# Thirty-two bytes in front of the activations: the activations stand 96 bytes from the weights, modulo 256, in place of 64

## The chip, the cores and the metric

One core of one Trainium2 chip runs the kernel. The metric is the device time of one execution in microseconds (us); less is better. All times below are of this one core.

## What is computed

The reference is a stack of four transformer-like layers in float32 on 256 tokens of 1024 channels. Two layers of a first kind mix tokens by a retention, a short convolution and a 31-tap convolution; two of a second kind mix by an mLSTM, a sparse attention and a differential attention. Each mixes through gates, and each is followed by a gated feed-forward block. Cut to what matters here:

```python
for l in range(2):                                # first kind
    h = rmsnorm(x, norm_mix_pre[l])
    proj = h @ w_in[l]                            # 1024 x 7168
    ...                                           # three branches, each ends in a 512 x 1024 product
    x = x + rmsnorm(merged @ w_o[l], norm_mix_post[l])
    h = rmsnorm(x, norm_ffn_pre[l])
    up = causal_dwconv(h @ w_up[l], ffn_conv_w[l])
    f = (silu(gate) * val) @ w_down[l]            # 2816 x 1024
    x = x + rmsnorm(f, norm_ffn_post[l])
for l in range(2):                                # second kind, likewise
    ...
```

Nearly all of the work is products of activations with weights that are each used once.

## The kernel before

**The stream of weights.** All weight matrices are cut on the host into blocks of 128 x 128 and packed, in the order of use, into chunks of eight blocks (512 KB). SyncE loads a chunk into a tile `wraw` (four buffers). A float32 weight goes to the tensor engine as the sum of two parts in the format float32r: ScalarE rounds the chunk into `whi` (line 326), and VectorE subtracts to get the rest into `wlo` (line 415, called from `Weights.ensure`). `whi` and `wlo` have four buffers each.

**The products.** `Gen.job` runs one product of the plan. For a weight block (kind "B") the weights are stationary (128 x 128) and 256 tokens of activations are moving. Activations have two parts too, so a block costs three matmuls: hi x `whi`, lo x `whi`, hi x `wlo`, all recorded under line 403. Activations are `hh`, `hl` (a whole normed input), `yh`, `yl` (a branch's output, or the first part of a norm), `fh`, `fl` (the feed-forward's middle) and `ckh`, `ckl` (a low-rank input of the sparse attention). A few products (kind "A") have the roles exchanged: the activations are stationary and 512 columns of weights move. Where `job` meets a chunk that is not split (`yw`, `wraw`), and in the sums of squares (`sqt`, `ones`, `cst`), the operands are plain float32.

**Work beside the products.** Generators (`spawn`, `side`) issue the attention, convolution and norm steps between the products. The program's order is fixed when it is built.

**Where tiles lie.** Each tile pool takes a stretch of every partition's memory, in the order in which pools are made, and a tile starts at the next multiple of 32 bytes. The pool `weights` is first, then `consts`, then `state` (the pool `self.xpool`), and behind these come the pools of each stage. In the built program all buffers of `wraw`, `whi` and `wlo` start at 128 modulo 256 bytes, and `x`, `yh`, `yl`, `sqt`, `hh`, `hl`, `fh` and `fl` at 192. Inside a tile, a token tile is 1024 bytes long and a weight block 512, so that the distance from a stationary block of weights to the activations that move against it is 64 bytes modulo 256 in every matmul on these tiles. `ckh` and `ckl` start at 32; their distance from the weights is 160.

```python
self.wpool = ctx.enter_context(tc.tile_pool(name="weights", bufs=1))
self.cpool = ctx.enter_context(tc.tile_pool(name="consts", bufs=1))
self.xpool = ctx.enter_context(tc.tile_pool(name="state", bufs=1))
...
self.x = self.xpool.tile([P, KD, T], F32, name="x")
...
todo = [(0, 0), (0, 1), (1, 0)] if len(ws) == 2 else [(0, 0)]
for j, (a, b) in enumerate(todo):
    self.mm(o, ws[a], xs[b], start=j == 0 and k == 0 and t % 2 == 0,
```

Of the kernel before, what the change touches and what calls it, by code (L numbers as in the profile page):

```python
# [11 lines left out]
F32 = mybir.dt.float32  # L12
# [5 lines left out]
P = 128  # L18
# [28 lines left out]
# norms after which the first chunks of weights and what they meet go unsplit  # L47
WHOLE = (1, 2, 3, 4)
# tiles of a product that ends a chain, the last ones apart
COLUMNS = ((0, 2), (2, 2), (4, 2), (6, 1), (7, 1))  # L50
# gates and products of the branches, in their order
# [8 lines left out]
def ffn_up(arr, l):  # L60
    """Gate and value tiles side by side; the first two products take four tiles."""
    t = [[_cols(i * P, P), _cols(FF + i * P, P)] for i in range(KF)]
    return [(arr, (l,), "B", KD, c) for c in [t[0] + t[1], t[2] + t[3]] + t[4:]]


def plan():
    """The weights in the order in which the tensor engine takes them: (array, index, kind,
    k tiles, columns), kind "B" by column tiles of 128 and "A" by rows of 512."""
    jobs = []

    def seg(arr, idx, nk, off, n, step=256):
        for i in range(0, n, step):
            jobs.append((arr, idx, "B", nk, [_cols(off + i + j, P) for j in range(0, step, P)]))

    def last_singly(arr, idx, nk):
        seg(arr, idx, nk, 0, D - 256)
        seg(arr, idx, nk, D - 256, 256, P)

    for l in range(DEPTH):
        seg("w_in", (l,), KD, OFF1["cfb"], 512, 512)  # L80
        seg("w_in", (l,), KD, OFF1["cfa"], 512, 512)
        for s, n in (("q", 256), ("k", 256)):
            seg("w_in", (l,), KD, OFF1[s], n)
        jobs.append(("w_in", (l,), "A", KD, _cols(OFF1["v"], 512)))
        for s, n in (("scc", 512), ("scx", 512), ("scb", 512), ("g", 512)):
            seg("w_in", (l,), KD, OFF1[s], n)
        for what, b in BRANCHES1:
            if what == "g":
                seg("w_in", (l,), KD, OFF1["gate"] + b * D, D)
            else:  # L90
                seg(("w_ret_out", "w_sc_out", "w_cf_out")[b], (l,), 4, 0, D)
        last_singly("w_o", (l,), KD)
        jobs += ffn_up("w_up", l)
        last_singly("w_down", (l,), KF)
    for l in range(DEPTH):
        w = "w_in_2"
        misc = np.full(P, -1)
        misc[:64] = _cols(OFF2["ik"], 64)
        misc[64:72] = _cols(OFF2["mif"], 8)
        misc[72:76] = _cols(OFF2["iw"], 4)  # L100
        jobs.append((w, (l,), "B", KD, [_cols(OFF2[s] + j, P) for s in ("iq", "ckv") for j in (0, P)]))
        seg(w, (l,), KD, OFF2["mqk"], 512, 512)
        jobs.append((w, (l,), "B", KD, [misc]))
        seg(w, (l,), KD, OFF2["mqk"] + 512, 512)
        jobs.append((w, (l,), "A", KD, _cols(OFF2["mv"], 512)))
        seg(w, (l,), KD, OFF2["mo"], 512)
        seg(w, (l,), KD, OFF2["dq"], 512)
        seg(w, (l,), KD, OFF2["dk"], 512)
        jobs.append((w, (l,), "A", KD, _cols(OFF2["dv"], 512)))
        seg("dsa_w_kv_up_2", (l,), 2, 0, 512)  # L110
        jobs.append(("dsa_w_kv_up_2", (l,), "A", 2, _cols(512, 512)))
        seg(w, (l,), KD, OFF2["sq"], 512)
        for what, b in BRANCHES2:
            if what == "g":
                seg(w, (l,), KD, OFF2["gate"] + b * D, D)
            else:
                seg("w_branch_2", (l, b), 4, 0, D)
        seg("w_out_2", (l,), KD, 0, D)
        jobs += ffn_up("w_gate_up_2", l)
        if l + 1 < DEPTH:  # L120
            seg("w_down_2", (l,), KF, 0, D)
        else:
            last_singly("w_down_2", (l,), KF)
    return jobs
# [48 lines left out]
def pack_params(inputs=None):  # L173
    """Per-channel parameters, channels on partitions: (offsets, array)."""
    off, parts = {}, []
# [37 lines left out]
def make_consts():  # L213
    """Tables that depend on shapes alone: (offsets, array [128, n])."""
    off, parts = {}, []
# [55 lines left out]
def whole_chunks():  # L271
    """The chunks that go to the tensor engine as float32, unsplit."""
    out, n, i = set(), 0, 0
    for _, _, kind, nk, cols in plan():
        if kind == "B" and len(cols) == 4:
            if i // 2 in WHOLE:
                out.add(n // CB)
            i += 1
        n += nk * (len(cols) if kind == "B" else 4)
    return out  # L280


class Weights:
    """The stream of weights: loads ahead, then each chunk as the sum of two float32r parts."""
# [13 lines left out]
    def cuts(self, c):  # L298
        """The first chunk comes in halves."""
# [44 lines left out]
class Gen:  # L344
    SLACK = 4000

    def __init__(self, ctx, tc, aps):
# [15 lines left out]
        self.idle = None  # L363
        self.x = self.xpool.tile([P, KD, T], F32, name="x")
# [82 lines left out]
    def split(self, hi, lo, src):  # L447
        """src as the sum of its float32r rounding and of the exact rest."""
# [3 lines left out]
    def behind(self, engine):  # L452
        """What is traced here is issued after the engine's last urgent instruction."""
# [21 lines left out]
    def side(self):  # L475
        """Steps of the tasks beside the products, as far as the vector engine keeps up."""
# [13 lines left out]
    def job(self, evac, mov, needs=(), scale=None, last=False, spare=None):  # L490
        """The next product of the plan. mov(k) gives the two parts of the activations' tile k;
        scale, per token, is for activations that were not normalised yet; spare gives tiles."""
# [3 lines left out]
        if kind == "B":  # L496
            n = len(cols)
            accs = [self.acc() for _ in range(-(-n // 2))]
            if self.idle is not None:
                # only to keep the tensor engine's clock up while it waits  # L500
# [4 lines left out]
            for k in range(nk):  # L505
                xs = mov(k)
                for t in range(n):
# [4 lines left out]
                    # a start clears the marks of its whole bank: the first product of a bank has it  # L512
# [32 lines left out]
    def swap(self, out, src):  # L545
        """src with the halves of each 64 channels exchanged"""
# [3 lines left out]
    def rows(self, r):  # L550
        # r in DRAM, from where a row goes to many partitions
# [4 lines left out]
    def spread(self, out, row):  # L556
        """a row on all the partitions of out"""
        self.nc.sync.dma_start(out, row.to_broadcast(list(out.shape)))

# [31 lines left out]
    def rstd(self, pool, ps, scale, name):  # L591
        """1 / sqrt(scale * ps + eps)"""
# [6 lines left out]
    def sumsq(self, out, last, hold):  # L599
        """Over channels, on every partition: the sum of the squares of the eight tiles, which it  # L600
        takes by pairs, the last two also one by one (send). The first ones are added up before.
        With hold the tensor engine gets them together at the end."""
# [37 lines left out]
    def start_norm(self, g, l, folded=4):  # L640
        """Takes x by pairs of tiles (feed) for a norm whose scale per token comes last."""
# [20 lines left out]
    def end_norm(self, sd=None):  # L662
        """What the first products take, with their scale, and what the others take."""
# [38 lines left out]
    def branches(self, order, bufs, pool, mov, gate_load, needs, ys, done):  # L702
        """The sum over branches of gate * (branch output times its matrix), as two parts. A gate
        sigmoid(z) comes as tanh(z / 2), its double less 1."""
# [31 lines left out]
    def post_norm(self, zg, sums, gpre, l):  # L736
        """x += normalised zg; then the next norm's input. With s the root mean square of z, what
        the norm sees is u = s * x + zg, s times the new x."""
# [23 lines left out]
    def unscale(self, sd):  # L762
        """x out of u"""
# [10 lines left out]
    def out_proj(self, mov, g, l):  # L774
        """Four products whose columns are scaled by g, with the sum of their squares."""
# [11 lines left out]
    def first_mix(self, l, norm):  # L787
        dmov, rs, whole, mov = norm
        nc = self.nc
        with ExitStack() as st:  # L790
# [6 lines left out]
            def new_y(b):  # L797
                """Buffers for a branch's output, once those of the one before last are free."""
# [13 lines left out]
            # conformer convolution  # L812
# [65 lines left out]
            # retention  # L878
# [44 lines left out]
            # short convolution  # L923
# [133 lines left out]
    def residual(self, mov, gpre, l):  # L1057
        """x += four products; then the next norm's input."""
# [17 lines left out]
    def second_mix(self, l, norm):  # L1076
        dmov, rs, whole, mov = norm
        nc = self.nc
        with ExitStack() as st:
# [11 lines left out]
            def new_y(b):  # L1091
                """Buffers for a branch's output, once those of the one before last are free."""
# [14 lines left out]
            def rope(o):  # L1107
                """Rotates two tiles in place."""
# [6 lines left out]
            # indexer  # L1115
# [63 lines left out]
            # key/value rank  # L1179
# [33 lines left out]
            def q_task(sqs, dst, rq):  # L1213
                """rotation of the queries, and their scale per token and head"""
# [39 lines left out]
            # mLSTM queries and keys  # L1254
# [29 lines left out]
            # mLSTM gates  # L1284
# [102 lines left out]
            # attention with a softmax: sets of (queries, keys) of 64 channels  # L1387
            def softmax_group(q, k, rq, t, grp, bias, p, sums):
                """p = exp(scores - max) for the queries of tile t, sums its row sums. A group is
                sets in the same half of the partitions, one a tile."""  # L1390
# [22 lines left out]
            def transposed(p):  # L1413
                """p by keys: for each set its blocks of keys"""
# [18 lines left out]
            def ahead(q, k, rq, t, bias):  # L1433
                """The groups of tile t with their softmax, one group ahead."""
# [49 lines left out]
            def diff(l=l):  # L1484
                init = 0.8 - 0.6 * math.exp(-0.3 * l)
                for t in range(2):
                    yt = tl([P, 512], "yt", tag="yt", bufs=3)
                    for (half, tiles), p, sums in ahead(dq, dk, rq_d, t, None):
# [5 lines left out]
                        # both maps in one, up to the first one's sums  # L1494
# [44 lines left out]
            # differential attention  # L1539
# [22 lines left out]
            # sparse attention: keys and values out of the rank  # L1562
# [72 lines left out]
```

## Time and profile before

| | before |
|---|---|
| time, median of 3 runs | 1789.86 us (1789.58 to 1791.06) |
| span of the profiled execution | 1789.1 us |
| granted TensorE clock, mean | 1.000 of full speed |
| PE (matmul) busy | 1777.4 us, 99% of the span |
| PEld (weight load) busy | 1729.2 us, 97% |
| VectorE (DVE) busy | 1363.0 us, 76% |
| ScalarE (ACT) busy | 1111.0 us, 62% |
| DMA | 322.52 MB, mean 180 GB/s |

The span runs from the first to the last instruction of one profiled execution; it lies 0.8 us under the median of the runs. A matmul's record lasts longer than the time until the next one starts, since matmuls are pipelined; what counts in a stretch is how many fit into it.

### The profile page before, as it was taken

The page shows a single profiled execution, that of the slowest core. Times are in us where ns is not written, and L with a number is a line of the kernel's source. Part 1 is how long each engine was busy: PE and PEld are TensorE (multiplying, and loading weights), DVE is VectorE, ACT ScalarE, POOL GpSimd, SP SyncE. Part 2 cuts the span into 40 slices and gives each one's busy share as a digit, 9 for nine tenths or more (in the row PEclk, how much of TensorE's full clock was granted, in tenths as well). Part 3 has the DMA queues.
Part 4 walks back from the last instruction along what each step waited for, and adds up shares of the span by engine and source line. Part 5 has one row for each costly group of instructions (what it writes and reads, how often), then busy time and mean ns, then how long its engine had stood idle before and what let it go on. Part 6 is the DMA issues. An engine that isn't in the chain of part 4 may idle for free.

```text
span 1789.1 us, 35765 instructions
## 1 busy us (share of the span) xinstructions
PE 1777.4 (99%) x14462; PEld 1729.2 (97%) x14462; DVE 1363.0 (76%) x2082; ACT 1111.0 (62%) x1787; POOL 70.2 (4%) x144
## 2 busy tenths in 40 slices
PE   8999999999999999999999999999999999999999
PEld 8999999999999999999998999999999999999999
DVE  8988679865999769884887877865569887677553
ACT  7575468755666567765576666654457666655542
POOL 0000000000000000000022100000000310000000
PEclk9999999999999999999999999999999999999999
DMA  7555546554655546555465644565555664356663
GB/s 265 191 171 179 187 154 200 188 187 164 210 168 188 177 138 204 189 189 188 137 195 177 201 142 139 168 207 194 189 186 180 199 201 139 124 177 200 193 196 132
DMA packets 94648, 322.52 MB, mean 180 GB/s; under 512 B 12257, under 2 KB 16913, under 8 KB 94482
## 3 DMA queue, kind: packets, MB, share of 16 engines
q1 hardware_dynamic: 91010, 314.15, 53.9%
q0 software_dynamic: 3328, 6.09, 1.1%
q8 instruction: 113, 1.85, 0.4%
q14 instruction: 53, 0.43, 0.1%
q10 hardware_dynamic: 144, 0.00, 0.0%
HBM read 312.80 MB, written 1.10 MB: 175 GB/s over the span
## 4 chain that ended last, share of the span: by engine, by line
PE 97%; DVE 1%; DMA 1%; issue 0%; ACT 0%; POOL 0%; SPq 0%; DVEq 0%; ACTq 0%; POOLq 0%
PE acc L403 90%; PE sp L403 6%; PE sp L408 1%; DMA tmp<-dq 0%; DMA Wm<-rows 0%; DMA x<-x 0%; DVE wlo L415 0%; DVE sc L1167 0%; DVE x L415 0%; DVE m L1166 0%; DVE yw L420 0%; ACT sd L445 0%; DVE dq L415 0%; ACT whi L326 0%; POOL tmp L548 0%
## 5 line engine op out<-in xcount | busy, mean ns | idle before, releaser
L326 ACT ACTIVATE whi<-wraw 128x1024 fp32r<-128x1024 f32 (+1 forms) x575 | 606.7, 1057 | 535.9 <-PE acc L403 367.8
L415 DVE TENSOR_TENSOR wlo<-wraw,whi 128x1024 fp32r<-128x1024 f32 (+1 forms) x575 | 699.0, 1220 | 282.9 <-ACT whi L326 281.3
L403 PE MATMUL acc<-hh,whi 128*128 128x256 f32 x2832 | 791.4, 280 | 0.0
L403 PE MATMUL acc<-hl,whi 128*128 128x256 f32 x2832 | 790.8, 280 | 0.0
L403 PE MATMUL acc<-hh,wlo 128*128 128x256 f32 x2832 | 789.9, 280 | 0.0
L403 PEld LDWEIGHTS acc<-hh,whi 128*128 128x128 f32 x2832 | 531.0, 188 | 5.5 <-issue 3.7
L403 PEld LDWEIGHTS acc<-hl,whi 128*128 128x128 f32 x2832 | 531.7, 188 | 1.9 <-issue 1.2
L403 PEld LDWEIGHTS acc<-hh,wlo 128*128 128x128 f32 x2832 | 531.4, 188 | 1.1 <-issue 0.8
L403 PE MATMUL acc<-yh,whi 128*128 128x256 f32 x1280 | 269.7, 284 | 6.2 <-ACT whi L326 6.2
L403 PE MATMUL acc<-yh,wlo 128*128 128x256 f32 x832 | 231.3, 283 | 0.0
L403 PEld LDWEIGHTS acc<-yh,whi 128*128 128x128 f32 x1280 | 210.5, 190 | 7.1 <-ACT whi L326 6.2
L403 PE MATMUL acc<-fh,wlo 128*128 128x256 f32 x704 | 196.0, 278 | 0.0
L403 PE MATMUL acc<-fl,whi 128*128 128x256 f32 x704 | 195.6, 278 | 0.0
L403 PE MATMUL acc<-fh,whi 128*128 128x256 f32 x704 | 195.5, 278 | 0.0
L403 PEld LDWEIGHTS acc<-yh,wlo 128*128 128x128 f32 x832 | 155.8, 189 | 0.4
L403 PEld LDWEIGHTS acc<-fh,wlo 128*128 128x128 f32 x704 | 132.3, 188 | 0.0
L403 PEld LDWEIGHTS acc<-fl,whi 128*128 128x128 f32 x704 | 132.2, 188 | 0.0
L403 PEld LDWEIGHTS acc<-fh,whi 128*128 128x128 f32 x704 | 132.0, 188 | 0.0
L403 PE MATMUL acc<-yl,whi 128*128 128x256 f32 x384 | 108.2, 282 | 0.0
L403 PEld LDWEIGHTS acc<-yl,whi 128*128 128x128 f32 x384 | 72.1, 188 | 0.2
L445 ACT ACT_TABLE_LOAD x50 | 64.2, 1283 | 5.5 <-DVE Wm L426 3.0
L420 DVE SCALAR_TENSOR_TENSOR up<-z,prm,up 128x254 f32<-128x254 f32 (+1 forms) x128 | 55.3, 479 | 0.0
(282 smaller groups left out, 1815.2 us busy)
## 6 DMA issues: line engine op xcount, KB each, us to landing
wraw<-stream SPq DMA_DIRECT2D x581, 512.0 KB, 3.6
kr<-rows SPq DMA_DIRECT2D x32, 64.0 KB, 3.0
dec<-decay SPq DMA_DIRECT2D x2, 768.0 KB, 4.3
x<-x SPq DMA_DIRECT2D x4, 256.0 KB, 6.3
rf<-rows SPq DMA_DIRECT2D x8, 128.0 KB, 3.5
tmp<-dq POOLq DMA_DIRECT2D x16, 64.0 KB, 3.8
Wm<-rows SPq DMA_DIRECT2D x8, 128.0 KB, 3.6
tmp<-dk POOLq DMA_DIRECT2D x16, 64.0 KB, 3.9
```

The costliest lines, as they stand in the source:

```text
L326: nc.scalar.activation(h[:, s], r[:, s], AF.Copy)
L403: return self.nc.tensor.matmul(out, lhsT, rhs, start=start, stop=stop, **kw)
L408: return self.nc.tensor.transpose(out, in_, self.c("ident")[:k, :k])
L415: self.recent = self.nc.vector.tensor_tensor(out=out, in0=a, in1=b, op=op)
L420: return self.nc.vector.scalar_tensor_tensor(out, a, s, b, op0=op0, op1=op1)
L445: return self.nc.scalar.activation(out, in_, f, **kw)
```

## The change

A tile of 8 float32 numbers (32 bytes in each partition) is allocated at the start of the pool `state`, in front of `x`. Nothing writes or reads it. Comments and docstrings go at the same time, which leaves the built instructions alone.

```diff
@@ -361,6 +361,8 @@
         self.t_x = [None]
         self.urgent = {}
         self.idle = None
+
+        self.xpool.tile([P, 8], F32, name="xpad")
         self.x = self.xpool.tile([P, KD, T], F32, name="x")
         xin = aps["x"].rearrange("p (k t) -> p k t", k=KD)
         self.coff, nco, _ = make_consts()
```

In the two built programs every engine has the same instructions in the same order, on tiles of the same shapes; only addresses differ. The weights, `cst`, `prm` and `ones` stay where they were. Everything from `x` on, in the pool `state` and in the pools behind it, lies 32 bytes further on. So `x`, `yh`, `yl`, `sqt`, `hh`, `hl`, `fh`, `fl` start at 224 modulo 256 and move against weights at a distance of 96; `ckh` and `ckl` start at 64, a distance of 192. With the roles exchanged (kind "A") the weights, moving, lie 192 bytes (modulo 256) from `hh` and `hl` before and 160 after, and from `ckh` and `ckl` 96 before and 64 after.

## Rows read from the trace of the kernel before

**Rows 1.** The page: busy time, and the chain that ended last.
```profile
PE 1777.4 (99%) x14462; PEld 1729.2 (97%) x14462; DVE 1363.0 (76%) x2082; ACT 1111.0 (62%) x1787; POOL 70.2 (4%) x144
...
PE 97%; DVE 1%; DMA 1%; issue 0%; ACT 0%; POOL 0%; SPq 0%; DVEq 0%; ACTq 0%; POOLq 0%
PE acc L403 90%; PE sp L403 6%; PE sp L408 1%; DMA tmp<-dq 0%; DMA Wm<-rows 0%; DMA x<-x 0%; DVE wlo L415 0%; DVE sc L1167 0%; DVE x L415 0%; DVE m L1166 0%; DVE yw L420 0%; ACT sd L445 0%; DVE dq L415 0%; ACT whi L326 0%; POOL tmp L548 0%
```

**Rows 2.** Groups of matmuls: count, busy us, mean ns of one, idle before.
```profile
L403 PE MATMUL acc<-hh,whi 128*128 128x256 f32 x2832 | 791.4, 280 | 0.0
...
L403 PE MATMUL acc<-yh,whi 128*128 128x256 f32 x1280 | 269.7, 284 | 6.2 <-ACT whi L326 6.2
L403 PE MATMUL acc<-yh,wlo 128*128 128x256 f32 x832 | 231.3, 283 | 0.0
L403 PE MATMUL acc<-fh,wlo 128*128 128x256 f32 x704 | 196.0, 278 | 0.0
...
L403 PE MATMUL acc<-yl,whi 128*128 128x256 f32 x384 | 108.2, 282 | 0.0
```

**Rows 3.** Four windows of 160 us, one in each feed-forward: busy us (instructions), clock, DMA.
```profile
core 0: us, PE busy (x) PEld busy (x) DVE busy (x) ACT busy (x) POOL busy (x), PEclk, DMA share, GB/s
253.00:413.00 160.00, 160.00 (x1361) 160.00 (x1360) 128.73 (x203) 112.66 (x191) 0.00 (x0) 1.00 0.58 190
700.00:860.00 160.00, 159.75 (x1333) 158.66 (x1332) 117.71 (x185) 107.31 (x185) 0.42 (x3) 1.00 0.55 179
1152.00:1312.00 160.00, 160.00 (x1414) 160.00 (x1413) 99.17 (x130) 82.83 (x118) 0.00 (x0) 1.00 0.62 196
1620.00:1780.00 160.00, 160.00 (x1414) 160.00 (x1413) 93.19 (x115) 75.85 (x104) 0.00 (x0) 1.00 0.59 187
```

**Rows 4.** Windows of PE alone: the eight stretches at the denser pace, and their sum.
```profile
17.50:25.00 7.50, 7.50 (x68) 1.00 0.59 191
...
1150.30:1316.90 166.60, 166.60 (x1472) 1.00 0.61 195
1343.60:1353.80 10.20, 10.20 (x93) 1.00 0.52 157
1613.00:1785.10 172.10, 172.10 (x1521) 1.00 0.57 184
sum 373.10, PE 373.10; mean PE 46.64
```

**Rows 5.** Timeline of PE where a dense stretch begins: start us, length us, what.
```profile
1149.34 1.03 PE L403 MATMUL sp<-sqt,ones 128*128 128x256 f32 x4
1150.02 0.58 PE L403 MATMUL acc<-yh,whi 128*128 128x256 f32 x2
1150.43 0.28 PE L403 MATMUL acc<-yh,wlo 128*128 128x256 f32 x1
```

**Rows 6.** Timeline of PE: a product on `ckh` and `ckl`, 160 bytes from the weights.
```profile
1433.87 0.28 PE L403 MATMUL acc<-ckl,whi 128*128 128x256 f32 x1
...
1435.06 0.28 PE L403 MATMUL acc<-ckh,wlo 128*128 128x256 f32 x1
1435.18 0.39 PE L403 MATMUL acc<-whi,ckh 128*128 128x512 f32 x1
```

**Rows 7.** Timeline of PE just ahead of that: short plain float32 products in a row.
```profile
1430.73 1.17 PE L403 MATMUL sp<-mv,Wm 128*128 128x129 f32 x9
1431.83 1.89 PE L403 MATMUL sp<-sqt,cst 128*8 128x256 f32 x8
```

**Rows 8.** Groups that prepare the weights, and what ended their waits.
```profile
L415 DVE TENSOR_TENSOR wlo<-wraw,whi 128x1024 fp32r<-128x1024 f32 (+1 forms) x575 | 699.0, 1220 | 282.9 <-ACT whi L326 281.3
L326 ACT ACTIVATE whi<-wraw 128x1024 fp32r<-128x1024 f32 (+1 forms) x575 | 606.7, 1057 | 535.9 <-PE acc L403 367.8 <-issue 125.8 <-DMA wraw<-stream 14.4
```

## The prediction

> **What bounds the kernel now.** I read the page first: PE is busy for 99% of the span, and the chain that ended last is PE for 97%, of which products with weights (`acc`, line 403) are 90% [rows 1]. So the time is the number of these matmuls times the pace at which they follow each other, and little else. The groups give the number: 2832 for each of three pairs on `hh` and `hl`, 704 for each of three on `fh` and `fl`, and 1280 + 832 + 384 on `yh` and `yl`, together 3 x 2832 + 3 x 704 + 2496 = 13,104 matmuls of 256 columns in float32r [rows 2].
>
> Next I asked whether they all run at one pace, with windows of one length laid into long unbroken products. They don't. A window of 160 us in the first feed-forward holds 1361 matmuls, in the third and fourth 1414 [rows 3]. A row counts every instruction that touches the window, and one lasts 0.28 us [rows 2], so two or three of each count belong to the edges. The paces are 160 / (1361 - 2.4) = 117.8 ns and 160 / (1414 - 2.4) = 113.35 ns. I call them slow and fast. PE is busy throughout in both, weight loads too, and the granted clock is 1.00, the 2.4 GHz level, in both. VectorE (129 against 99 us busy) and ScalarE are less loaded in the fast ones, but they hold up nobody there: the matmul groups on `hh` and `fh` have no idle time before them [rows 2, 3]. The DMA moves 196 GB/s in a fast window and 190 in a slow one, so it is no brake either.
>
> The third view is where the fast pace stands. Eight stretches have it, 373.1 us in all; two feed-forwards hold nearly everything (166.6 and 172.1 us), and within a stretch it never changes [rows 4]. It begins after an interruption: at 1149.34 us a sum of squares with plain float32 operands cuts the row of products, and what follows it is fast [rows 5]. 373.1 / 0.11335 = 3290 matmuls are fast; some 9,800 are not.
>
> So the same instruction, on tiles at the same distance modulo 256, settles into one of two rhythms and keeps it until something breaks in. Matmul and weight load run side by side, both read the same memory, and a rhythm that depends on the moment of restart looks like two streams of reads that get in each other's way more or less often. That is an inference; no row names a collision.
>
> **The change, part by part.** It removes nothing and adds no instruction. The order on every engine is that of before, so nothing is moved past a queue and no wait is added.
>
> The new tile costs no time: it has no instruction, and the highest tile still fits.
>
> All other engines' operands from `x` on lie 32 bytes further on. I price that at nothing: VectorE and ScalarE have 24% and 38% of the span free [rows 1], and the two steps in front of PE, the split of a chunk, wait for each other and for PE most of the time (283 us and 536 us idle ahead of them) [rows 8]. If a slower access made each 1% longer, the 699 us of `wlo` would grow by 7 us, spread over idle time; without that cover it would cost the 7 us.
>
> What is left is the distance of the moving activations from the stationary weights, 64 before and 96 after, in all 13,104 matmuls. No row has activations that move at 96 from the weights, so I bound the price by the paces that the trace shows.
> - The fast pace everywhere: 9,800 x (117.8 - 113.35) = 43.6 us less.
> - The slow pace everywhere: 3290 x 4.45 = 14.6 us more.
> - A third distance is in the trace. Eleven gaps on `ckh` and `ckl`, at 160, take 1435.18 - 1433.87 = 1.31 us, or 119 ns each [rows 6]. With this pace everywhere, 14.6 + 13,104 x 1.3 = 32 us more.
> - Weight loads alone set a floor. Nine short float32 products with a new stationary block each take 1.17 us, the last one 0.28 of it, so (1.17 - 0.28) / 8 = 111 ns [rows 7]. Below this none of these products can go, since each has its own weight load. At the floor everywhere: 43.6 + 13,104 x 2.3 = 74 us less.
>
> Plain float32 products of 256 columns go at (1.89 - 0.38) / 7 = 216 ns [rows 7], about half the rate of float32r; I leave them out of the sum, and with them the few products of 512 columns.
>
> The rule of the Trainium skill that speaks against the change is in "TensorE: Matmul & The Clock Gate", step-by-step part, on the weight load: the engine has two independent read ports, so "Loading the next tile's weights doesn't steal SBUF read bandwidth from the running matmul." By it no distance matters, and the sum is zero. The same page's isolated gap for 256 columns, 262 cycles at 2.4 GHz or 109 ns, would as an estimate make the products 13,104 x 7.5 = 98 us shorter than they are. The trace sides with neither figure: it has two paces, both longer.
>
> Which pace will 96 have? The trace shows that distance matters at all only through 64 (two paces) and 160 (one, slower, in few and short products), and a straight line between the two would put 96 at 117.4 ns, a little worse than today's mean of (3290 x 113.35 + 9,814 x 117.8) / 13,104 = 116.7. I don't take the line, because the paces go by steps: a stretch is fast or slow and never between. At 64 the kernel sits where a restart decides, and 32 bytes are 32/1024 of a moving operand, 113.35 x 32 / 1024 = 3.5 ns of its stream. That is most of the 4.45 ns between the rhythms, so I expect the new distance to have one rhythm nearly everywhere, not a mix. The fast one is 2 ns off the floor of the weight loads, that is, a rhythm in which hardly anything collides; and the moving stream, which passes through 1024 bytes while the weights pass through 512, starts with half as much lead again at 96. I take the fast one, by judgement more than by proof.
>
> The sum: 43.6 us, less some 4 us for the 3% of the chain that isn't PE, for products next to a break, and for the first mixes, where VectorE has little room and at a faster pace would be waited for. 40 us off a span of 1789.1 gives 1749, and with 0.8 us around it 1750 us. The median of the runs is 0.8 us above the profiled span, within the spread of the runs.
>
> **The rivals.**
> - *It ends slower: a worse rhythm everywhere.* Place: the same products. Price: 14.6 us at 117.8 ns, 32 us at the 119 ns of distance 160, thus 1804 to 1822 us. For it: 75% of the matmuls are at the slow pace today, and the only other distance seen is worse. Against it: those are 11 gaps after a break. It decides if fewer than a quarter of the products are fast. Chance 0.25.
> - *The mix is dealt anew.* The restart goes on deciding, and other stretches turn out fast. Each of the four feed-forwards is worth about 1500 x 4.45 = 6.7 us, so the time goes in such steps from 1804 to some 1770 us. For it: at 64 it is just so. Chance 0.18: 0.08 of it faster, 0.05 the same, 0.05 slower.
> - *The distance does nothing,* by the rule above: two independent read ports, and the two rhythms come from something else that the change leaves alone. 1790 us. For it: breaks are in the same places. Against it: `ckh` at another distance has a third pace. Chance 0.05.
> - *No collisions are left,* and the products run near the floor of the weight loads: 1716 us. For it: the fast pace is already within 2.3 ns. Against it: no float32r product in the trace does so. Chance 0.10.
>
> **How the numbers follow.** The forecast has 0.42 and gives 1750 us (its own range, from 1746 with no haircut to 1768 with half of the slow products turned fast). Faster by over 0.2% (3.6 us, about what a measurement of this kernel can tell) is 0.42 + 0.08 + 0.10 = 0.60; within 0.2%: 0.05 + 0.05 = 0.10; slower: 0.25 + 0.05 = 0.30. The range goes from 1735, between the full fast rhythm and the floor, to 1806, just past the slow rhythm everywhere. Outside lie most of the floor case and the half of the slower rival that follows distance 160, together about 2 in 10.
>
> **What would show it.** Right: windows of 160 us in the first and second feed-forward hold 1400 matmuls or more, at unchanged clock; the mean of a matmul on `hh` falls from 280 ns towards 276; no new wait in front of PE. Wrong in size: some of these windows still hold 1361. Wrong in sign: the third and fourth feed-forward hold 1361 or fewer. Wrong in mechanism: the counts are as before and the time has changed elsewhere, in waits of PE for `whi`, or on VectorE. The products on `ckh`, at 192 after, should change their 119 ns too if the distance is what matters.

## The result, and the profile after

The changed kernel takes 1831.86 us (median of 4 runs, 1831.44 to 1832.37), the kernel before 1789.72 us beside it (4 runs, 1789.53 to 1791.06). The ratio is 1.0234, with a 95% interval of 1.0221 to 1.0246. The change makes the kernel 42.1 us slower. That is above the range of the prediction, and on the side of its first rival.

The page of the kernel after: span, busy time, and the chain that ended last.

```profile
span 1830.2 us, 35765 instructions
...
PE 1818.8 (99%) x14462; PEld 1771.1 (97%) x14462; DVE 1364.6 (75%) x2082; ACT 1110.7 (61%) x1787; POOL 69.4 (4%) x144
...
PE 97%; DVE 1%; DMA 1%; ACT 1%; issue 0%; POOL 0%; SPq 0%; DVEq 0%; ACTq 0%; POOLq 0%
```

Against [rows 1], only PE's two rows moved, by 41.4 and 41.9 us. VectorE and ScalarE are busy for as long as before, on the addresses 32 bytes further on, and the chain is PE for 97% still. So the loss is inside PE's products.

The costliest groups of the kernel after. Line 403 of before is line 405 now, and line 415 is 417.

```profile
L326 ACT ACTIVATE whi<-wraw 128x1024 fp32r<-128x1024 f32 (+1 forms) x575 | 606.6, 1056 | 579.5 <-PE acc L405 396.9
L417 DVE TENSOR_TENSOR wlo<-wraw,whi 128x1024 fp32r<-128x1024 f32 (+1 forms) x575 | 698.4, 1218 | 316.1 <-ACT whi L326 314.2
L405 PE MATMUL acc<-hh,whi 128*128 128x256 f32 x2832 | 800.1, 283 | 0.0
...
L405 PE MATMUL acc<-yh,whi 128*128 128x256 f32 x1280 | 274.2, 286 | 6.6 <-ACT whi L326 6.6
```

The steps in front of PE last as long as in [rows 8] (1056 against 1057 ns, 1218 against 1220 ns), and their idle time has grown by 44 and 33 us, most of it waiting for PE or for each other. PE waits for `whi` about as long as before (6.6 against 6.2 us in [rows 2]). A matmul on `hh` has gone from 280 to 283 ns.

Four windows of 160 us, one in each feed-forward of the kernel after (busy us and instructions of each engine, clock, DMA):

```profile
core 0: us, PE busy (x) PEld busy (x) DVE busy (x) ACT busy (x) POOL busy (x), PEclk, DMA share, GB/s
260.00:420.00 160.00, 160.00 (x1336) 160.00 (x1335) 126.56 (x202) 111.28 (x189) 0.00 (x0) 1.00 0.56 184
705.00:865.00 160.00, 160.00 (x1336) 160.00 (x1335) 118.79 (x184) 107.94 (x183) 0.00 (x0) 1.00 0.57 188
1185.00:1345.00 160.00, 160.00 (x1334) 159.94 (x1333) 87.36 (x108) 75.84 (x106) 0.00 (x0) 1.00 0.56 185
1650.00:1810.00 160.00, 160.00 (x1336) 160.00 (x1335) 89.57 (x112) 74.38 (x104) 0.00 (x0) 1.00 0.55 185
```

Against 1361, 1333, 1414 and 1414 in [rows 3], the count is now 1334 to 1336 in all four: 160 / (1336 - 2.4) = 120.0 ns for each matmul, at the same granted clock. (The 1333 of before is a window with a break in it, of which its 158.66 us of weight loads tell.) The two rhythms are gone. One has taken their place, and it is worse than either.

To check this on all of them, I took the time from each start to the next start for every pair of neighbouring float32r matmuls of 256 columns in the trace, 12,868 pairs without those next to a break. The mean is 116.64 ns before and 119.97 after. 12,868 x 3.33 ns = 42.8 us, against 42.1 us measured: this is the whole difference. I call this mean the pace below.

The products on `ckh`, whose distance went from 160 to 192, as a timeline of PE in the kernel after:

```profile
1462.55 0.29 PE L405 MATMUL acc<-ckl,whi 128*128 128x256 f32 x1
...
1462.90 0.28 PE L405 MATMUL acc<-ckl,whi 128*128 128x256 f32 x1
...
1463.70 0.28 PE L405 MATMUL acc<-ckh,wlo 128*128 128x256 f32 x1
1463.81 0.39 PE L405 MATMUL acc<-whi,ckh 128*128 128x512 f32 x1
```

The same eleven gaps as in [rows 6] take 1463.81 - 1462.55 = 1.26 us, or 115 ns each, where [rows 6] has 119; the last eight of them take 1463.81 - 1462.90 = 0.91 us, or 114 ns each. The same 32 bytes made these products faster while they made the others slower. So it looks like the distance 96 that is slow, and 192 may be good.

### The profile page after: what moved, and what is told of

Read it like the earlier page. It is cut to its first block, busy times and chain, and to the rows that moved or that the text cites. A ratio compares the mean times of both kernels' runs of the same rounds, so it can differ in the third digit from the quotient of the medians.

```text
span 1830.2 us, 35765 instructions
## 1 busy us (share of the span) xinstructions
PE 1818.8 (99%) x14462; PEld 1771.1 (97%) x14462; DVE 1364.6 (75%) x2082; ACT 1110.7 (61%) x1787; POOL 69.4 (4%) x144
## 4 chain that ended last, share of the span: by engine, by line
PE 97%; DVE 1%; DMA 1%; ACT 1%; issue 0%; POOL 0%; SPq 0%; DVEq 0%; ACTq 0%; POOLq 0%
PE acc L405 90%; PE sp L405 6%; PE sp L410 1%; DMA tmp<-dq 0%; DMA x<-x 0%; DMA Wm<-rows 0%; DVE sc L1169 0%; ACT L447 0%; ACT whi L326 0%; DVE x L417 0%; DVE m L1168 0%; DVE yw L422 0%; ACT sd L447 0%; DVE wlo L417 0%; DVE dq L417 0%
## 5 line engine op out<-in xcount | busy, mean ns | idle before, releaser
L326 ACT ACTIVATE whi<-wraw 128x1024 fp32r<-128x1024 f32 (+1 forms) x575 | 606.6, 1056 | 579.5 <-PE acc L405 396.9
L417 DVE TENSOR_TENSOR wlo<-wraw,whi 128x1024 fp32r<-128x1024 f32 (+1 forms) x575 | 698.4, 1218 | 316.1 <-ACT whi L326 314.2
L405 PE MATMUL acc<-hh,whi 128*128 128x256 f32 x2832 | 800.1, 283 | 0.0
L405 PE MATMUL acc<-hh,wlo 128*128 128x256 f32 x2832 | 798.7, 283 | 0.0
L405 PE MATMUL acc<-yh,whi 128*128 128x256 f32 x1280 | 274.2, 286 | 6.6 <-ACT whi L326 6.6
L405 PE MATMUL acc<-yl,whi 128*128 128x256 f32 x384 | 108.8, 284 | 0.0
```

The source lines that it names most:

```text
L326: nc.scalar.activation(h[:, s], r[:, s], AF.Copy)
L405: return self.nc.tensor.matmul(out, lhsT, rhs, start=start, stop=stop, **kw)
L417: self.recent = self.nc.vector.tensor_tensor(out=out, in0=a, in1=b, op=op)
```

## The experiments

My theory after the result: the pace belongs to the distance between the stationary block and the moving operand, modulo 256 bytes, and 96 is among the worst. The rivals: it is the address of the activations themselves; or it is what other engines and the DMA do at the new addresses while PE runs.

**Everything shifted.** The 32 bytes go in front of the weights in place of the activations. All tiles then lie where they lie after the change, except that the weights have moved along, so that the distance is 64 again.

```diff
         self.wpool = ctx.enter_context(tc.tile_pool(name="weights", bufs=1))
+        self.wpool.tile([P, 8], F32, name="wpad")
 ...
-        self.xpool.tile([P, 8], F32, name="xpad")
```

> The 32 bytes stand in front of the weights instead of the activations: all tiles move by 32, the activations stand at 224 modulo 256 as in the change, but their distance from the weights is 64 again. If the distance sets the pace: 1790 us, as before, with the two rhythms of 113.3 and 117.8 ns back in the same stretches. If what costs is that the activations start at an odd multiple of 32 bytes, whatever the weights do: 1832 us and 120 ns throughout, as in the change.

Measured: 1790.43 us (10 runs), ratio to before 0.9999 (0.9990 to 1.0008). The windows of [rows 3] laid over this kernel, PE alone (busy us and instructions, clock, DMA):

```profile
253.00:413.00 160.00, 160.00 (x1361) 1.00 0.57 190
700.00:860.00 160.00, 159.75 (x1331) 1.00 0.52 178
1152.00:1312.00 160.00, 160.00 (x1415) 1.00 0.58 196
1620.00:1780.00 160.00, 160.00 (x1415) 1.00 0.58 187
```

Both rhythms are back, and in the same feed-forwards. The addresses by themselves cost nothing. The distance does.

**The same distance, 256 bytes further.** The pad is `[P, 72]`, 288 bytes.

> The unused tile has 288 bytes: a distance of 96 plus 256 from the weights. If only the distance modulo 256 counts: 1832 us and 120 ns, as with 32 bytes. If it is the distance itself, or the place of the activations in a larger unit, another pace, with 1790 us as likely as anything.

Measured: 1832.63 us (1831.82 to 1833.70), ratio 1.0236 (1.0221 to 1.0251), pace 119.97 ns. It is the changed kernel's time again, so the distance counts modulo 256, or modulo something that divides it.

**The other distances.** The pad is 128, 96, 64, 192, 160 or 224 bytes, for distances of 192, 160, 128, 0, 224 and 32; the edit is the one number in `[P, 8]`.

> The unused tile has 128 bytes: a distance of 192. With the change the low-rank products on ckh came to a distance of 192 and went at 113.3 ns. If the distance sets the pace of every float32r product alike: 113.3 ns nearly throughout, about 1790 - 43 = 1747 us. If the address of the activations alone counts (64 modulo 256, an even multiple of 32): as before, 1790 us.

> The unused tile has 96 bytes: a distance of 160. Before the change the low-rank products on ckh stood at 160 and went at 119 ns. If the distance sets the pace: 119 ns throughout, 1790 + 13100 x 2.3 ns = 1820 us. If an odd multiple of 32 bytes is what costs: 120 ns and 1832 us as in the change, the two lie within 0.7%, so the pace in the windows decides.

> The unused tile has 64 bytes: a distance of 128. Distances 64 and 192 have the same two rhythms (113.3 and 117.8 ns), 96 and 160 don't. If multiples of 64 share them: some 1770 to 1790 us, windows with one or the other rhythm. If the paces repeat after 128 bytes only, 128 is a new class with 0, its pace open (111 to 122 ns, 1716 to 1860 us) but the same as that of distance 0.

> The unused tile has 192 bytes: a distance of 0, both operands at 128 modulo 256. If the paces repeat after 128 bytes: the time of distance 128, within 1%. If they repeat after 256 only: any other. A plain picture of two streams that start at the same place and collide there would make it the slowest of all, over 1832 us.

> The unused tile has 160 bytes: a distance of 224, 32 short of 256. If the paces repeat after 128 bytes: 120.0 ns and 1832 us, as at 96. If they mirror (32 bytes on either side alike): as at 32, whatever that is. If the odd multiple of 32 is what costs: 119 to 120 ns, 1814 to 1832 us.

> The unused tile has 224 bytes: a distance of 32. If the paces repeat after 128 bytes: 118.8 ns and 1814 us, as at 160. If odd multiples of 32 cost alike: between 1814 and 1832 us. If neither: another time, and the paces depend on the distance modulo 256 without a shorter period.

| distance | time, us (median) | ratio to before (95%) | pace, ns | by pace, us |
|---|---|---|---|---|
| 0 | 1831.37 | 1.0230 (1.0215 to 1.0245) | 119.94 | 1832 |
| 32 | 1791.49 | 1.0008 (0.9998 to 1.0017) | 116.80 | 1792 |
| 64 (before) | 1789.72 | 1 | 116.64 | 1790 |
| 96 (after) | 1831.86 | 1.0234 (1.0221 to 1.0246) | 119.97 | 1833 |
| 128 | 1822.83 | 1.0182 (1.0165 to 1.0199) | 119.24 | 1823 |
| 160 | 1813.60 | 1.0126 (1.0109 to 1.0143) | 118.82 | 1818 |
| 192 | 1779.52 | 0.9943 (0.9929 to 0.9958) | 115.86 | 1780 |
| 224 | 1811.31 | 1.0118 (1.0103 to 1.0133) | 118.32 | 1811 |

The last column is 1789.9 + 12,868 x (pace - 116.64 ns). It meets the profiled run of every kernel within 2 us (at 160 that run took 1818.2 us, the slowest of its four), so nothing but the pace is needed for any of them. The table has no shorter period: 32 and 160 differ by 22 us, 96 and 224 by 21. (0 and 128 lie within the 1% that was set beforehand; they differ in their rhythms, 120.0 ns alone at 0, 118.7 and 120.0 ns at 128.) It has no simple slope either. At 0, 96 and 224 I find one rhythm, and at 32 one but for two short stretches at 117.8 ns; at 64, 128, 160 and 192 there are several, and a stretch keeps the one that it fell into. At 192 neither time that was expected came: the rhythms are the two of distance 64, in other places. The windows of that kernel, PE alone:

```profile
253.00:413.00 160.00, 160.00 (x1360) 1.00 0.55 188
680.00:840.00 160.00, 160.00 (x1361) 1.00 0.56 190
1140.00:1300.00 160.00, 160.00 (x1414) 1.00 0.60 194
1600.00:1760.00 160.00, 160.00 (x1361) 1.00 0.54 186
```

One of the four is fast here, two of them in [rows 3]. The kernel is 10 us faster than before all the same, since more of its other products are fast.

**PE alone.** This kernel, like the next three, computes nothing of the reference: it runs matmuls on float32r tiles while ScalarE, VectorE and the DMA have nothing to do. Weights and activations start at the same place modulo 256, and the moving operand is taken `d` bytes in. Each distance comes three times, each time after a break of a few plain float32 products; then come turns (odd matmuls with weights at distance 64, even ones at 0), 512 columns, and plain float32.

```python
for turn in range(3):
    for d in range(0, 256, 32):
        rest(4 + turn)
        o = acc(f"at{d}b")
        for i in range(120):
            k, b = i % 5, i % 15
            mm(o[:, :T], w[:, b * P:(b + 1) * P], a[:, d // 4 + k * T:d // 4 + k * T + T])
```

> Nothing of the reference is computed: after one load and four copies the tensor engine runs alone, with no work of ScalarE, VectorE or the DMA beside it. Runs of 120 float32r matmuls of 256 columns at each of the eight distances, three restarts each, then matmuls whose weights stand in turn at 64 and 0, then 512 columns, then plain float32. If the paces are an affair of weight load and moving operand: the paces of the eight kernels come back, 120.0 ns at 0 and 96, 113.3 or 117.8 at 64 and 192, 118.3 at 224, 116.7 at 32, 118.5 or 120 at 128, 117.5 to 120 at 160. If other engines' reads and writes or the DMA make the second party: one pace at all distances, the floor near 111 to 113 ns. In the turns: if a matmul is slowed by the weights that load beside it, those on weights at 64 (beside a load at 0) are longer than those on weights at 0; if by its own weights, the other way round. Plain float32: 216 ns at all distances.

Windows of 12 us of this kernel, PE alone. In order: distances 64, 96 and 192 of the first turn; 0, 32, 64, 96, 128, 160 and 192 of the second.

```profile
46.00:58.00 12.00, 12.00 (x104) 1.00 0.01 1
62.00:74.00 12.00, 12.00 (x102) 1.00 0.00 1
110.00:122.00 12.00, 12.00 (x104) 1.00 0.00 1
142.00:154.00 12.00, 12.00 (x102) 1.00 0.00 1
159.00:171.00 12.00, 12.00 (x105) 1.00 0.01 1
175.00:187.00 12.00, 12.00 (x108) 1.00 0.01 1
191.00:203.00 12.00, 12.00 (x102) 1.00 0.01 1
207.00:219.00 12.00, 12.00 (x103) 1.00 0.00 1
223.00:235.00 12.00, 12.00 (x105) 1.00 0.01 1
240.00:252.00 12.00, 12.00 (x105) 1.00 0.00 1
```

The DMA moves 1 GB/s and the order of the distances is that of the kernel: 102 at 0 and 96, 105 at 32, and at 64 once 104 and once 108. Taken from the starts of 120 matmuls, without the first 15 behind a break, the paces are 120.0 ns at 0 and in all three turns at 96, 116.7 at 32, 117.8, 113.3 and 117.8 at 64, 118.7 and twice 120 at 128, 117.3 to 118.7 at 160, 117.8 in all three at 192, and 118.3 at 224. No other engine is needed for any of it: the second rival falls, too.

Two groups of the same kernel tell the turns apart, and two more show plain float32 (count, busy us, mean ns of one, idle before):

```profile
L45 PE MATMUL ownfar<-a,w 128*128 128x256 f32 x180 | 42.7, 282 | 0.0
L45 PE MATMUL ownnear<-a,w 128*128 128x256 f32 x180 | 42.1, 277 | 0.0
...
L45 PE MATMUL plain0b<-fa,fw 128*128 128x256 f32 x40 | 8.8, 379 | 0.0
...
L45 PE MATMUL plain96b<-fa,fw 128*128 128x256 f32 x40 | 8.8, 379 | 0.0
```

With weights in turn at 0 and at 64 the two kinds take 118.3 and 115.0 ns from start to start, 116.67 in the mean, half way from 120.0 to 113.3. So a matmul seems to have a pace by its own weights, not by those of the matmul behind it. But the weights two matmuls on stand at the same distance as its own, and a load that runs that far ahead would give the same; this stays open. Plain float32 takes 215.9 ns a record at all eight distances, and two records a matmul: the program has 20 of them at each distance, the row counts 40.

**Three distances at once.** A block's three matmuls need not share one distance: `whi`, `wlo`, `hh` and `hl` could be placed apart. This kernel tries all 8 x 8 x 8 settings of the distances of hi from `whi`, hi from `wlo` and lo from `whi`, 45 matmuls each, with a break before each.

```python
mm(o[:, :T], wh, hi)    # hi stands d bytes from wh
mm(o[:, :T], wh, lo)    # lo stands f bytes from wh
mm(o[:, :T], wl, hi)    # hi stands e bytes from wl
```

> Nothing of the reference is computed: the tensor engine runs the kernel's three matmuls a block (hi x whi, lo x whi, hi x wlo) with the three distances set one by one, 512 settings of 45 matmuls after a break each. If the pace follows each pair's own distance, the mean of a setting is the mean of the three single paces, between 113.3 and 120 ns, and no setting beats 113.3. If a setting locks as a whole, some mixed settings go at 113.3 ns or below where no single distance does so safely, and such a setting in the kernel would give 1747 us.

Measured: the settings average 118.3 ns and none goes below 113.33. Just three reach that, (64, 64, 64), (192, 64, 192) and (192, 192, 192), with nothing but 64 and 192 in them; the next best has about 115.4. The mean of the three single paces predicts a setting's pace poorly (correlation 0.14). So a setting seems to lock as a whole, and no mix beat a single distance. Each setting was started once; whether some have a faster rhythm that this start missed is open.

**What picks the rhythm.** With 64 and 192 as the two distances that have a fast rhythm, one shorter matmul of `n` columns goes between runs of 36 full ones, for every `n` from 8 to 256 in steps of 8, in four turns.

```python
mm(ps[:, :n], w[:, :P], a[:, d // 4:d // 4 + n])
for i in range(36):
    k, b = i % 5, i % 15
    mm(o[:, :T], w[:, b * P:(b + 1) * P], a[:, d // 4 + k * T:d // 4 + k * T + T])
```

> Nothing of the reference is computed: the tensor engine alone, runs of 36 matmuls of 256 columns at a distance of 64 or 192, each behind one matmul of 8 to 256 columns. If the moment of restart picks between the two rhythms: the length of the short matmul decides, the same length gives the same rhythm in all four turns, and some lengths always give 113.3 ns. If the rhythm that held before goes on, or something outside the tensor engine picks: no relation to the length, and about one run in four fast, as in the kernel.

Measured: at 192, behind 112, 128, 144, 168, 184, 192, 200, 208 and 232 columns the next 36 go at 113.3 ns in all four turns; behind 120, 136, 152, 160, 176, 216, 224, 240, 248 and 256 they go at 117.8 in all four; up to 104 columns it varies. At 64 the slow rhythm holds behind every `n` from 24 up. This looks as if the columns of the short one decided at 192. But the order of `n` is the same in every turn, so that from 120 columns up each `n` met the same rhythm in all four: 128 always came behind a stretch at 117.8 ns, 136 always behind one at 113.3. Columns and the rhythm before are not told apart here.

**A product in two cuts.** If a short matmul turns the rhythm, so may a matmul that is cut into two of `n` and 256 - `n` columns, which a kernel can do at no loss of work. This kernel tries all cuts at 192 four times, and was meant to meet either rhythm twice.

```python
short(start)                # was to set the rhythm before
run("prior", 30)
short(n)
short(T - n, n)
o = run("then", 36)
```

> Nothing of the reference is computed: the tensor engine alone at a distance of 192. Thirty matmuls behind a short one of 120 columns (slow rhythm) or of 128 (fast), then one product in two cuts of n and 256 - n columns, then 36 whole ones. If the last cut's length alone picks the rhythm, as the single short matmul did: what follows is at 113.3 ns where 256 - n is 112, 128, 144, 168, 184, 192, 200, 208 or 232, out of either rhythm, and at 117.8 otherwise. If the moment within the run picks: other lengths, or a dependence on the rhythm before, and then no cut is safe.

Measured: the columns of a short one don't pick the rhythm by themselves. Two of the trials, with PE merged into runs (start and length in us; 36 matmuls take 4.49 us in the slow rhythm and 4.33 in the fast one, 30 take 3.75 and 3.64):

```profile
400.59 4.49 PE L45 MATMUL then<-a,w 128*128 128x256 f32 x36
404.92 0.22 PE L45 MATMUL short<-a,w 128*128 128x128 f32 x1
404.98 3.64 PE L45 MATMUL prior<-a,w 128*128 128x256 f32 x30
...
416.55 4.33 PE L45 MATMUL then<-a,w 128*128 128x256 f32 x36
420.72 0.22 PE L45 MATMUL short<-a,w 128*128 128x128 f32 x1
420.77 3.75 PE L45 MATMUL prior<-a,w 128*128 128x256 f32 x30
```

The same 128 columns turn 117.8 ns into 113.3 in the first and 113.3 into 117.8 in the second. Over 122 trials, the fast rhythm gave way to the slow one behind 128 columns 52 times of 52 and behind 120 columns 57 of 57; the slow one gave way to the fast one 6 times of 9 and 4 of 4. So nearly all cuts were met in the slow rhythm, whatever the short one ahead. Out of it, 102 of 112 led to 113.3 ns, among them 64 + 192, 128 + 128 and 144 + 112 in 4 of 4. Some do not: 88 + 168 led to the slow rhythm out of both, 160 + 96 and 200 + 56 kept the one before. 96 + 160 is one of few cuts that met both rhythms, twice each, and led to 113.3 ns every time. A cut costs 0.10 to 0.14 us.

**Cuts in the kernel.** The kernel at distance 192 gets one matmul in cuts of 96 and 160 columns in every fourth product, 62 cuts in all; and the changed kernel, at 96, the same 62 cuts for comparison.

```diff
+        self.njob = 0
 ...
+        self.njob += 1
 ...
                     for j, (a, b) in enumerate(todo):
+                        if self.njob % 4 == 0 and k == 1 and t == j == 0 and len(todo) == 3:
+                            for s in (slice(0, 96), slice(96, T)):
+                                self.mm(o[:, s], ws[a], xs[b][:, s], start=False, stop=False, skip_group_check=True)
+                            continue
```

> The activations at a distance of 192, and in every fourth product one matmul is done in two cuts of 96 and 160 columns; the tensor engine alone came out of this cut in the fast rhythm whichever it had been in. 62 cuts at some 0.11 us are 7 us. If a cut sets the rhythm in the kernel too: nearly all stretches at 113.3 ns, 1779.5 - 12868 x 2.4 ns + 7 = 1756 us, and the feed-forwards hold 1400 matmuls and more in 160 us. If the order hi, lo, hi of the kernel, or the loads beside it, keep the cut from setting it: 1780 + 7 = 1787 us, with the mix of before.

> The changed kernel (distance 96) with the same 62 cuts: there is one rhythm of 120.0 ns there, so a cut has nothing to set and this run gives its price. 1832 + 7 = 1839 us. If a cut breaks the 120 ns too, as a second rhythm at 96 that no restart found so far: less than 1832.

Measured: 1765.78 us at 192 (1764.02 to 1766.72), ratio to before 0.9862 (0.9847 to 0.9877); 1838.03 us at 96, ratio 1.0265 (1.0248 to 1.0282). At 96, where there is no other rhythm to turn to, the pace stays at 119.95 ns and the cuts cost 1838.0 - 1831.9 = 6.2 us, or 0.1 us each. At 192 the same cuts bring the pace from 115.86 to 114.27 ns: 12,868 x 1.59 = 20.5 us, less the 6.2, is the 13.7 us between 1779.5 and 1765.8 within 1 us. This version beats both kernels, but the 1756 us that were expected, with nearly all stretches fast, did not come.

The timeline of PE around one cut at 192, the plain matmul ahead of it, the cut (two records in one row) and some behind it:

```profile
273.83 0.28 PE L405 MATMUL acc<-hh,whi 128*128 128x256 f32 x1
...
277.95 0.28 PE L405 MATMUL acc<-hh,wlo 128*128 128x256 f32 x1
278.07 0.35 PE L405 MATMUL acc<-hh,whi 128*128 128x96 f32 x2
278.26 0.32 PE L405 MATMUL acc<-hl,whi 128*128 128x256 f32 x1
...
279.11 0.28 PE L405 MATMUL acc<-hh,wlo 128*128 128x256 f32 x1
...
280.47 0.28 PE L405 MATMUL acc<-hh,wlo 128*128 128x256 f32 x1
```

From 273.83 to 277.95 lie 35 gaps of 117.7 ns, from 279.11 to 280.47 twelve of 113.3. This cut turned the rhythm. Another, of the same columns, did not:

```profile
1147.64 0.35 PE L405 MATMUL acc<-hh,whi 128*128 128x96 f32 x2
...
1148.10 0.28 PE L405 MATMUL acc<-hh,whi 128*128 128x256 f32 x1
...
1170.24 0.28 PE L405 MATMUL acc<-hh,wlo 128*128 128x256 f32 x1
```

From 1148.10 to 1170.24 lie 188 gaps of 117.8 ns, as ahead of this cut. Of the 14 cuts that met the slow rhythm, 8 turned it, 5 left it slow, and behind one too few matmuls follow to tell; none is seen to turn a fast one slow. Why five failed, where PE alone had 2 of 2 out of the slow rhythm, is open. The windows of this kernel, PE alone, show what it still misses:

```profile
253.00:413.00 160.00, 160.00 (x1405) 1.00 0.56 192
680.00:840.00 160.00, 159.75 (x1384) 1.00 0.55 188
1140.00:1300.00 160.00, 160.00 (x1401) 1.00 0.57 195
1600.00:1754.00 154.00, 154.00 (x1354) 1.00 0.56 190
```

1405 and 1401 are near the 1414 of a window that is fast throughout. They are short of it by their slow beginnings, up to the cut at 278.07 in the first and past the cut of 1147.64 to the next one at 1170.36 in the third; the last window, 6 us shorter, begins slow too, up to 1619.8 us. The 1384 are no slow stretch: that window runs into the break at 833.4 us, and plain float32 products fill it from there. After each break the rhythm is dealt anew and stays slow, where it came out so, until a cut turns it, and the next cut is up to four products away.

## Why the prediction was wrong

**What bounds the kernel** was read rightly. PE's products are the time before and after [rows 1, 2], and one number, the pace, accounts for every one of the kernels above.

**"An inference; no row names a collision."** The inference that the distance is at work held: the kernel with everything shifted brought the time back, and PE alone shows the same paces by distance. That something collides in the memory is still only inferred. What collides, and why 96 and 0 give 120.0 ns, is open.

**The rest of the change at nothing** was right. VectorE and ScalarE are busy as before, and no wait took their place.

**"I expect the new distance to have one rhythm nearly everywhere, not a mix"** was right: all four windows agree, and so do all three restarts with PE alone. But it was right by luck. The reason given, that 32 bytes shift the stream by most of the 4.45 ns between the rhythms, would hold for every other step of 32 bytes too, and at 128, 160 and 192 there are several rhythms.

**"I take the fast one, by judgement more than by proof"** is the step that failed: 96 has one rhythm at 120.0 ns, worse than both, which added 42.8 us where the forecast took 43.6 us off. The choice rested on two thoughts. One was that a longer lead of the moving stream means fewer collisions. The table denies it: lead and pace have no order, 192 is the best and 96, half way to it, as bad as 0. The other was that a stretch "is fast or slow and never between", by which I dismissed the straight line through 64 and 160. That holds for the rhythms at 64, but other distances have paces between those two (116.7 ns at 32) and beyond them (118.3 at 224, 120.0 at 96). The two rhythms that I had seen were not the two to choose from. The line would have had the sign right and the size wrong, 117.4 ns in place of 120.0. What the trace of before gave was no direction at all, and one row [rows 6] against the change.

**"It ends slower: a worse rhythm everywhere"** is the rival that came true. Its mechanism was right and its price was too low. The upper bound was the 119 ns of [rows 6], for 32 us; the measured 120.0 ns cost 42 us. The 119 ns was no mistake of reading, as the kernel at 160 has a pace of 118.8. It was taken as the end of the scale because it was the worst that the trace showed. The range did not even take this bound in: it ended at 1806, just past the 1804 of the slow rhythm everywhere.

**The other rivals.** *The mix is dealt anew* is what 192 did, not 96. *No collisions are left* found no support: none of 512 settings went below 113.33 ns, and 111 ns was never reached. Nor does [rows 7] show that the 111 ns are a floor of weight loads, as the prediction read it: its records have 129 columns, and at the 215.9 ns of a plain float32 record of 256 columns that alone is 108.8 ns. The price of this rival and the lower end of the range, 1735, rested on that reading. The rate of plain float32 was misread beside it: two records make a matmul, so one of 256 columns takes 431.7 ns, near four times the 116.6 of float32r and not about twice. It entered no sum. *The distance does nothing* fell with PE alone. The sentence of the Trainium skill behind it ("TensorE: Matmul & The Clock Gate", step-by-step part) says that the next load of weights takes no read bandwidth from the running matmul. If nothing else hung on the distance, the eight distances would have one pace by it. For float32r and 256 columns the runs show 113.3 to 120.0 ns by distance, and the measurement decides; that it is the read bandwidth which is lost is not shown. Plain float32, at 215.9 ns a record everywhere, agrees with it.

## What to carry to other kernels

Where float32r matmuls of 256 columns with a new stationary block each bound a kernel, the distance of the moving operand from the stationary one, modulo 256 bytes, was worth 3% here between its ends (1779.5 us at 192 against 1831.9 at 96; 10 us against the kernel before), and one unused tile sets it: measure all eight multiples of 32, since neighbours tell nothing of each other. Where a distance has two rhythms, count instructions in windows of one length, for the rhythm can often be turned: at 192 a single matmul cut into 96 and 160 columns turned the slow one into the fast one in 8 of 13 cases in the kernel, and 62 such cuts were worth 13.7 us. When a trial tells what sets a state, vary the state before it as well: four equal answers in the same order of trials were not four proofs. And when a trace shows two values of a quantity whose cause isn't known, a third setting may lie outside both; price it beyond them.

## What the runs showed of the hardware

- The pace of float32r matmuls of 256 columns depends on the distance between stationary and moving operand modulo 256 bytes, with no other engine at work. The paces are sharp; among them are 113.33, 116.67, 117.78, 118.3 and 120.0 ns, which at the granted 2.4 GHz are 272, 280, 282.7, 284 and 288 clocks.
- At 64 and 192 two paces are stable, 113.33 and 117.78 ns, and over a thousand matmuls in a row keep the one that they fell into. At 192 one shorter matmul changes it: with PE alone, 120 or 128 columns turned the fast one slow 109 times of 109, and a slow one fast 10 times of 13. By what rule is open.
- One plain float32 matmul of 256 columns is two records of 215.9 ns each, at every distance (20 matmuls, x40).
- With 512 moving columns the matmuls take 226.7 ns at 0, 228.8 at 64 and 233.3 to 234.4 elsewhere (40 matmuls each, PE alone). Here 0 is the best distance, for 256 columns it is among the worst.
